# Zero-padded low parts of queries, attention heads in pairs, and the gate projected inside its attention

## The chip, the core and the metric

The kernel runs on one core of a Trainium2 chip. TensorE (PE in the profile) multiplies; VectorE (DVE), ScalarE (ACT) and GpSimd (POOL) do the rest; SyncE (SP) and ACT issue transfers. The metric is device microseconds of one execution, lower is better.

## What is computed

Two transformer blocks of two layers each, 1024 features, batch 1: a latent segment of 512 tokens and a context segment of 256. The first block has an RWKV7 layer (a recurrence over tokens) and then a differential attention layer; each layer of the second block has a feed-forward half step, a mixer of four kinds of heads (one kind is latent attention), and another half step. The change touches the two attentions. In short:

```python
# differential attention, 8 heads of 2 components of 64 features, values of 128
q, k = rope(rms_norm(proj_q)), rope(rms_norm(proj_k))     # [T, 8, 2, 64]
s = einsum("bqhcd,bkhcd->bchqk", q, k_all) * 64**-0.5      # 512 queries, 768 keys
p = softmax(s); attn = p[:, 0] - lam * p[:, 1]
y = rms_norm(einsum("bhqk,bkhe->bqhe", attn, v_all), subln) * (1 - lam_init)
y = (y * silu(proj_g)) @ w_out

# latent attention, 4 heads, 64 + 32 rotary features, values of 64
q = rms_norm(cq) @ w_uq                                    # cq has 192 features
k, v = split(rms_norm(ckv) @ w_ukv)                        # ckv has 128 features
o = softmax(q @ k_all.T * 96**-0.5) @ v_all
```

## The kernel before

Large products run on pairs of a high part and a low part in a rounded type (`fp32r`): `mm3` (L89) issues three products for each piece (high x high, high x low, low x high), and a `WStream` (L64) loads a piece of weights, lets ACT make its high part and DVE or POOL its low part. The smaller products run on plain fp32; the trace has two records for each of those, one for a transpose and one for an `fp32r` product. In the trace a form like `64*128 64x512` says that 64 rows by 128 columns of the PE array are used, for 512 columns streamed.

**Differential attention** is `da_heads` (L766). For each of 8 heads j, `queries_keys(j)` (L835) projects queries (`psq`) and keys (`psk`), norms and rotates them. The two components have 64 features each. For component c, `qq[:, c]` holds the high part of the query on all 128 rows, twice; `kk[:, c]` holds the high part of the keys on the component's own 64 rows and the low part on the other 64. So one product over 128 rows gives high x (high + low). The low part of the query, `ql`, has both components stacked, and its product takes only the 64 rows of the component:

```python
nc.tensor.matmul(o, qq[:, c, qc], kk[:, c, k0 : k0 + kn], start=True, stop=False)         # L919
nc.tensor.matmul(o, ql[cpn, qc], kk[cpn, c, k0 : k0 + kn], start=False, stop=True)        # L920
```

The keys' norm factors (`rk`, 12 columns) are spread over rows by 12 products of 64 columns of the array into `bck`. At its end `queries_keys` projects the gate (`psg`, 24 products of 512 columns, then tanh on ACT). `attend(j)` (L901) has, for each half of the queries (q2), two blocks of 128: scores, maximum on DVE (L921), exponential on ACT (L925), the weighted difference of both components on DVE (L930, L931), six transposes (`ptr`, L936), high and low parts of them, and then 18 products with the values (`po`). `values(g)` (L816) projects the values of two heads. The program writes, for each j, `values` of the pair, `queries_keys(j)`, and then `attend(j - 1)`.

**Latent attention** is `mix_attention` (L1371), called by `mix` (L1113) once for the context (layer 0 alone) and in both layers for the latent tokens. For each of 4 heads, `prepare` makes queries (`psuq`: a product over 128 rows and one over 64) and keys (`psuk`, 64 columns of the array), and `attend` takes blocks of 128 queries: scores (`pssc`), softmax, transposes (`mptr`), and the product with the values (`mpo`, 64 columns of the array, six products over 256 queries). For latent tokens two heads are in flight; for the context one.

**What sets the order.** The program is built with a planner that simulates the engines and writes every engine's instructions in an order of its own; the code's order is only where it starts, and buffers bound what it may move. The context segment of the second block (names with a `c`: `chi`, `clo`, `cx`; its feed-forward products are `pab` and `pf`) does not depend on the first block and is spread by the planner over the recurrence (about 500 to 1,600 us) and the differential attention (1,750 to 2,390 us). The latent mixers of the two layers run at about 2,867 to 3,046 and 3,860 to 4,075 us, beside projections of their other heads (`psz`, `pssv`, `psf`, `psfo`) and the output projection (`pf`).

Of the kernel before, what the change touches and what calls it, by code (L numbers as in the profile page):

```python
# [153 lines left out]
def ada(S, which, l, pool, psp, bufs=3, cols=None):  # L154
    """modulation vectors, 1024 columns at a time -> S.mod[(which, l)]; a generator of pieces"""
# [25 lines left out]
def make_gs(S, dst, mcols, gname, l):  # L181
    """dst[:, k, j] = g[k] * (1 + scale[k, j])"""
# [67 lines left out]
        # mixing factors  # L250
# [93 lines left out]
def rwkv_streams(S, st):  # L344
    """-> tw (the low-rank inputs, to be filled) and stage1(j, k, r): a generator that leaves the streams and the triangular inverses of the head pair j in DRAM"""
# [35 lines left out]
    def stage1(j, k_, r_):  # L381
# [5 lines left out]
        for hf in range(2):  # L387
# [18 lines left out]
            for d in range(2):  # L406
# [40 lines left out]
                # strictly triangular system matrices  # L447
# [81 lines left out]
def rwkv_scan(S, s1, start, fill):  # L529
    nc, tc, A = S.nc, S.tc, S.A  # L530
    with ExitStack() as st:
# [28 lines left out]
        # [.., pair of chunks, L | R, 4 blocks of 64]: L = I k k I for an odd and an even chunk, R = P r r P for an even and an odd one  # L560
# [7 lines left out]
        def group(j, d, c0, El):  # L568
            """transition matrices of the four chunks from c0 on"""
# [62 lines left out]
        def loadV(j, gi):  # L632
            """[.., direction, pair of chunks, parity, (head, v)]: V and the incoming states"""
# [10 lines left out]
        def stage2(j):  # L644
# [42 lines left out]
            # readout  # L687
# [48 lines left out]
def rwkv_out(S):  # L736
    """output projection, residual, x and context -> S.d_x (feature-major)"""
# [25 lines left out]
# ---------------------------------------------------------------- differential attention layer  # L763


def da_heads(S):  # L766
    """reads S.d_x, leaves the gated heads in S.d_yda"""
    nc, tc, A = S.nc, S.tc, S.A
    with ExitStack() as st:
# [16 lines left out]
        with tc.tile_pool(reuse_waits="tile", name="dax", bufs=1) as xp:  # L786
# [5 lines left out]
            # lambda  # L792
# [42 lines left out]
        def queries_keys(j):  # L835
            """q, k normed and roped, the gate: -> tiles for attend(j)"""
# [29 lines left out]
            ql = tp.tile([128, NLAT], F32R, tag="ql", name="ql", bufs=2)  # L866
            kk = tp.tile([128, 2, NT], F32R, tag="kk", name="kk", bufs=2)
            for t in (qs, ks[:, NCTX:]):
# [6 lines left out]
                if t is qs:  # L875
                    for c in range(2):
# [15 lines left out]
            # gate  # L892
# [3 lines left out]
            th = tp.tile([128, NLAT], F32, tag="th", name="th", bufs=2)  # L896
            nc.scalar.activation(out=th, in_=pg, func=AF.Tanh, scale=0.5)
            nc.vector.scalar_tensor_tensor(out=th, in0=th, scalar=1.0, in1=pg, op0=ALU.add, op1=ALU.mult)
            return qq, ql, kk, rq, th

        def attend(j, qq, ql, kk, rq, th):  # L901
# [3 lines left out]
            for q2 in range(2):  # L905
                PTh = ap.tile([128, 6, 256], F32R, tag="PTh", name="PTh")
                PTl = ap.tile([128, 6, 256], F32R, tag="PTl", name="PTl")
                for qi in range(2):
# [5 lines left out]
                    for c in range(2):  # L914
                        cpn = slice(64 * c, 64 * c + 64)
# [8 lines left out]
                        e = ap.tile([128, NT], F32, tag=f"e{c}", name=f"e{c}", bufs=2)  # L924
# [8 lines left out]
                    for i0 in (0, 3):  # L933
# [4 lines left out]
                        split(S, PTh[:, i0 : i0 + 3, ql_], PTl[:, i0 : i0 + 3, ql_], pv)  # L938
                q2s = slice(256 * q2, 256 * q2 + 256)
# [34 lines left out]
class Path:  # L974
    """one token segment of the second block: n tokens, modulation column j (0 latent, 1 context)"""
# [5 lines left out]
def halves(P, n, count, name):  # L981
    """count accumulators of n columns, two to a bank where they fit"""
# [8 lines left out]
def da_out(S, E, tp, after):  # L991
    """output projection and residual of the attention layer, for the latent tokens"""
# [9 lines left out]
def project(S, E, src, gate, after=None, x=None, order=range(8)):  # L1002
    """x += gate * (h @ w), 1024 features to 1024"""
# [5 lines left out]
def add(S, E, src, x, kc, gate, order, after=None):  # L1009
    """x += gate * (h @ w); before a norm, half of the features in token halves, so that the norm of one runs beside the other"""  # L1010
# [12 lines left out]
def ffn(S, E, l, which, hook=None, after=None):  # L1023
    """x += gate * swiglu(h) with h = hi + lo"""
# [34 lines left out]
class Norm:  # L1059
    """the norm of the latent tokens by halves"""  # L1060
# [21 lines left out]
class Final(Norm):  # L1082
    """the last norm, to the output"""
# [18 lines left out]
def gelu2(S, dst, ps, n, tp, bufs=True):  # L1102
    """2 * gelu(ps) (tanh form)"""
# [9 lines left out]
def mix(S, E, l):  # L1113
    """the mixed heads of one segment: hi + lo (normed input) -> hi + lo (heads, before the output projection)"""
# [7 lines left out]
    with ExitStack() as st:  # L1122
# [4 lines left out]
        def keep(name, w=n):  # L1127
            """a projection that a mixer needs later: context ones wait in DRAM"""
# [22 lines left out]
        # latent and key projections  # L1151
# [6 lines left out]
        if not kv_only:  # L1158
            cq0, cq1 = keep("cq0"), keep("cq1")
            sq0 = tp.tile([128, n], F32, tag="t0", name="sq0", bufs=2)  # L1160
            sq1 = tp.tile([128, n], F32, tag="a0", name="sq1")

# [19 lines left out]
        if not kv_only:  # L1182
            away("cq0", cq0)
            if not lat:
                nc.sync.dma_start(S.d_st["cq1"][0:64, :n], cq1[0:64])
            pss = E.at.tile([128, 512], F32, "mm", "pssq")
            for i in range(nt):
                tk = slice(128 * i, 128 * i + 128)
                mm(nc, pss[:, i : i + 1], sq0[:, tk], S.ones[:, 0:1], True, False)
                mm(nc, pss[:, i : i + 1], sq1[0:64, tk], S.ones[0:64, 0:1], False, True)  # L1190
# [3 lines left out]
        # rope of the shared key part  # L1194
# [37 lines left out]
        # pooling input  # L1232
# [10 lines left out]
        # gating units  # L1243
# [23 lines left out]
        # Fourier input  # L1267
# [7 lines left out]
        def put(ch, ps, scale=None):  # L1275
            """columns of the mixed heads, split for the output projection"""
# [10 lines left out]
        # pooling mixer  # L1287
# [24 lines left out]
        # spatial gating  # L1312
# [27 lines left out]
        # Fourier mixer  # L1340
# [30 lines left out]
def mix_attention(S, E, l, zp, tp, cq0, cq1, ckv, kr, rq, mcs, nk, fetch):  # L1371
# [7 lines left out]
    if not lat:  # L1379
        cq1 = zp.tile([128, n + 32], F32, tag="fb", name="cq1f")[:, :n]  # L1380
        nc.sync.dma_start(cq1[0:64], S.d_st["cq1"][0:64, :n])
# [9 lines left out]
    for i in range(nb):  # L1391
        kt = kr if i == 0 else zp.tile([128, NK], F32, name="mk")
        if i:
            nc.vector.tensor_copy(kt[64:96, :], kr[64:96, :])
        kts.append(kt)

    def prepare(hh):
        """the queries and keys of a head"""
        wuq = tp.tile([128, 2, 128], F32, tag=tag("wuq", "w1"), name="wuq", bufs=nb)
        nc.sync.dma_start(wuq, A["wuq"][l][:, :, 128 * hh : 128 * hh + 128])  # L1400
# [495 lines left out]
```

## Time and profile before

| | |
|---|---|
| median of 3 runs (lowest, highest) | 4460.86 us (4459.17, 4468.64) |
| span of the profiled execution | 4460.2 us |
| PE busy | 4203.0 us (94%) |
| DVE, ACT, POOL busy | 2410.0, 1633.5, 1502.2 us (54%, 37%, 34%) |
| mean granted PE clock | 0.961 of 2.4 GHz |

The profiled execution lies inside the range of the runs, and its span is 0.7 us below their median, so what lies around the span is left out. A duration in the trace is that of one instruction; matmuls overlap, so what a product costs PE is the distance from its start to the next start. A row of the timeline merges neighbours of one kind ("x16"), from the first start to the last end.

### The profile page before, as it was taken

Reading aid. Unit: us, or ns where it says so; the run is one execution under the profiler, and the core shown is the slowest. Engines: PE = TensorE matmul, PEld = TensorE weight load, DVE = VectorE, ACT = ScalarE, POOL = GpSimd, SP = SyncE. Lnnn points to the kernel's source line nnn. Section 1 sums busy time; section 2 is a strip of 40 time slices with the busy share of each in tenths; the row PEclk is TensorE's granted clock in tenths of the full one; section 3 lists DMA queues with packets and bytes.
Section 4 is the critical chain, followed back from the end, with each engine's and each line's share of the span. In section 5 each row is a group of like instructions: output and inputs, shape, how many; then the busy total and the mean of one; then the engine's idle time right before and its main releaser. Section 6 shows DMA issues by size and latency. Waiting matters only on the chain.

```text
span 4460.2 us, 70923 instructions
## 1 busy us (share of the span) xinstructions
PE 4203.0 (94%) x27642; PEld 3466.0 (78%) x27642; DVE 2410.0 (54%) x4716; ACT 1633.5 (37%) x3020; POOL 1502.2 (34%) x1187
## 2 busy tenths in 40 slices
PE   7999888999999997999998999999999999999998
PEld 5667767889768897778877888867888888857887
DVE  4677888645655435566665535554333523555434
ACT  3333333334424443444443323343222322343222
POOL 3444445356414752332223333211222222301221
PEclk9999978999999998999998999999999999999999
DMA  7775455565876653222214333311332232301332
GB/s 254 255 241 162 127 169 165 176 200 183 271 251 202 219 186 105 67 74 68 75 45 144 103 107 96 122 46 47 95 96 95 94 95 92 117 29 60 102 99 81
DMA packets 347119, 581.42 MB, mean 130 GB/s; under 512 B 96416, under 2 KB 194720, under 8 KB 345632
## 3 DMA queue, kind: packets, MB, share of 16 engines
q1 hardware_dynamic: 205856, 402.31, 28.1%
q10 hardware_dynamic: 140928, 174.58, 12.8%
q8 instruction: 218, 3.57, 0.3%
q14 instruction: 117, 0.96, 0.1%
HBM read 509.26 MB, written 67.50 MB: 129 GB/s over the span
## 4 chain that ended last, share of the span: by engine, by line
PE 78%; DVE 14%; DMA 4%; issue 2%; ACT 2%; POOL 0%; SPq 0%; ACTq 0%; DVEq 0%; POOLq 0%
PE pab L90 9%; PE pab L91 9%; PE pab L92 9%; PE pf L90 6%; PE pf L91 6%; PE pf L92 6%; PE aps L47 2%; PE ps L47 2%; DVE tmp L478 2%; DVE B L479 2%; PE pch L47 2%; PE psg L47 1%; PE psw L47 1%; PE psu L90 1%; PE mpo L47 1%
## 5 line engine op out<-in xcount | busy, mean ns | idle before, releaser
L81 POOL TENSOR_TENSOR wl<-wr,wh 128x512 fp32r<-128x512 f32 (+3 forms) x719 | 1090.4, 1527 | 2293.2 <-ACT wh L78 2100.7
L78 ACT ACTIVATE wh<-wr 128x512 fp32r<-128x512 f32 (+3 forms) x918 | 696.8, 766 | 1490.0 <-PE pab L91 585.7
L91 PE MATMUL pab<-llo,wh 128*128 128x512 f32 (+1 forms) x1472 | 561.4, 382 | 3.8 <-DVE llo L141 3.8
L90 PE MATMUL pab<-lhi,wh 128*128 128x512 f32 (+1 forms) x1472 | 557.9, 382 | 6.6 <-ACT lhi L139 6.5
L92 PE MATMUL pab<-lhi,wl 128*128 128x512 f32 (+1 forms) x1472 | 560.1, 381 | 0.0
L90 PE MATMUL pf<-gh,wh 128*128 128x256 f32 (+1 forms) x1328 | 451.9, 343 | 33.3 <-DVE cx L1018 20.1
L91 PE MATMUL pf<-gl,wh 128*128 128x256 f32 (+1 forms) x1328 | 449.2, 340 | 0.5 <-DVE gl L151 0.4
L92 PE MATMUL pf<-gh,wl 128*128 128x256 f32 (+1 forms) x1328 | 448.9, 341 | 0.9 <-POOL wl L81 0.9
L81 DVE TENSOR_TENSOR wl<-wr,wh 128x1024 fp32r<-128x1024 f32 (+2 forms) x199 | 237.6, 1195 | 211.1 <-ACT wh L78 209.0
L90 PE MATMUL pab<-chi,wh 128*128 128x256 f32 x1056 | 314.5, 299 | 18.3 <-DVE nt L138 8.6
L91 PEld LDWEIGHTS pab<-llo,wh 128*128 128x128 f32 x1472 | 278.9, 189 | 57.2 <-DVE llo L141 4.5
L90 PEld LDWEIGHTS pab<-lhi,wh 128*128 128x128 f32 x1472 | 276.9, 189 | 59.7 <-ACT lhi L139 7.9
L92 PEld LDWEIGHTS pab<-lhi,wl 128*128 128x128 f32 x1472 | 279.0, 190 | 52.3
L92 PE MATMUL pab<-chi,wl 128*128 128x256 f32 x1056 | 308.7, 295 | 6.5 <-POOL wl L81 6.1
L90 PEld LDWEIGHTS pf<-gh,wh 128*128 128x128 f32 x1328 | 254.9, 193 | 71.7 <-issue 16.8
L91 PE MATMUL pab<-clo,wh 128*128 128x256 f32 x1056 | 308.4, 293 | 0.0
L91 PEld LDWEIGHTS pf<-gl,wh 128*128 128x128 f32 x1328 | 256.5, 193 | 33.0 <-issue 1.7
L92 PEld LDWEIGHTS pf<-gh,wl 128*128 128x128 f32 x1328 | 256.2, 193 | 29.5 <-POOL wl L81 1.1
L90 PEld LDWEIGHTS pab<-chi,wh 128*128 128x128 f32 x1056 | 209.7, 199 | 32.3 <-issue 15.7
L1044 DVE TENSOR_TENSOR fth<-fth,pab 128x512 f32<-128x512 f32 (+1 forms) x154 | 88.0, 572 | 260.6 <-PE pab L92 258.7
L1018 DVE SCALAR_TENSOR_TENSOR x<-pf,lgt,x 128x512 f32<-128x512 f32 (+1 forms) x144 | 98.9, 690 | 233.9 <-PE pf L92 233.6
L1043 DVE SCALAR_TENSOR_TENSOR fth<-fth,pab 128x512 f32<-128x512 f32 (+1 forms) x154 | 87.7, 569 | 250.6 <-ACT fth L1042 250.2
(504 smaller groups left out, 9014.2 us busy)
## 6 DMA issues: line engine op xcount, KB each, us to landing
adaw<-in_adaw SPq DMA_DIRECT2D x192, 512.0 KB, 5.4
wr<-in_w SPq DMA_DIRECT2D x176, 512.0 KB, 3.5
wr<-in_w ACTq DMA_DIRECT2D x344, 256.0 KB, 3.0
wr<-in_w SPq DMA_DIRECT2D x96, 384.0 KB, 3.2
wr<-in_rwin SPq DMA_DIRECT2D x32, 512.0 KB, 5.0
wr<-in_w ACTq DMA_DIRECT2D x104, 128.0 KB, 2.1
dS<-strm SPq DMA_DIRECT2D x32, 384.0 KB, 2.7
dL<-str SPq DMA_DIRECT2D x32, 384.0 KB, 3.2
```

The source lines that it names most:

```text
L47: nc.tensor.matmul(out, lhsT, rhs, start=start, stop=stop)
L78: nc.scalar.activation(out=hv, in_=rv, func=AF.Copy)
L81: eng.tensor_tensor(out=lv, in0=rv, in1=hv, op=ALU.subtract)
L90: nc.tensor.matmul(ps, whi, xhi, start=first, stop=False)
L91: nc.tensor.matmul(ps, whi, xlo, start=False, stop=False)
L92: nc.tensor.matmul(ps, wlo, xhi, start=False, stop=last)
L478: el.tensor_tensor(out=tv, in0=B[L, 0:s, s : s + 1].to_broadcast([96, s, n]), in1=B[L, s : s + 1, s + 1 :].to_broadcast([96, s, n]), op=AL ...
L479: el.tensor_tensor(out=B[L, 0:s, s + 1 :], in0=B[L, 0:s, s + 1 :], in1=tv, op=ALU.add)
L1018: S.nc.vector.scalar_tensor_tensor(out=E.x[:, f, sl], in0=ps[:, sl], scalar=gate[:, f : f + 1], in1=E.x[:, f, sl], op0=ALU.mult, op1=ALU.add)
L1043: nc.vector.scalar_tensor_tensor(out=th, in0=th, scalar=1.0, in1=pa, op0=ALU.add, op1=ALU.mult)
L1044: nc.vector.tensor_tensor(out=th, in0=th, in1=pb, op=ALU.mult)
```

## The change

It does six things.

- `ql` gets a tile for each component's own rows, with zeros on the other 64 rows (set once, on POOL); the low product runs over all 128 rows. There are as many products of the same widths as before.
- The norm factors of the keys are first copied 64 times each into a tile of 768 columns (`spread`, one ACT instruction for each head), which six transposes bring to `bck`, in place of 12 products.
- The gate is projected by a new function `gate(j)`, called in `attend(j)` between the first half's softmax and its product with the values. `values` is called after `attend(j - 1)`, with two buffers instead of three.
- Latent attention takes two heads at a time: one product gives the keys of both (128 columns of the array), and the products with the values alternate between the two heads, one writing rows 0 to 63 of `mpo`, the other 64 to 127. Both halves are then copied out together.
- `cq1` and its square are padded with zeros from 64 to 128 rows.
- In `norm_mod` the tile `nh` has as many buffers as `nsq`, or shares its buffer where there is one. The copy of the shared key part moves from DVE to POOL.

```diff
+def spread(S, pool, cols, n, tag):
+    w = pool.tile([128, n, 64], F32, tag=tag, name="wide")
+    S.nc.scalar.activation(out=w, in_=cols.unsqueeze(2).to_broadcast([128, n, 64]), func=AF.Copy)
+    return w.rearrange("p n r -> p (n r)")
...
-            h = pool.tile([128, w], F32, tag="nh", name="nh")[:, :n]
+            h = pool.tile([128, w], F32, tag="nsq" if bufs == 1 else "nh", name="nh", bufs=bufs)[:, :n]
...
+        qls = [tp.tile([128, 2, NLAT], F32R, name=f"ql{i}") for i in range(2)]
+        for t in qls:
+            for c in range(2):
+                nc.gpsimd.memset(t[64 - 64 * c : 128 - 64 * c, c].bitcast(F32), 0.0)
...
-            vs = [[tp.tile([128, 6, 128], F32R, tag=t, name=t, bufs=3) for t in ("vh", "vl")] for _ in range(2)]
+            vs = [[tp.tile([128, 6, 128], F32R, tag=t, name=t, bufs=2) for t in ("vh", "vl")] for _ in range(2)]
...
-                        nc.vector.tensor_tensor(out=ql[own], in0=qs[own], in1=qq[own, c], op=ALU.subtract)
+                        nc.vector.tensor_tensor(out=ql[own, c], in0=qs[own], in1=qq[own, c], op=ALU.subtract)
+            wide = spread(S, tp, rk, 12, "sq")
...
-                    for h in range(2):
-                        mm(nc, bc[64 * h : 64 * h + 64, 128 * (i - i0) : 128 * (i - i0) + 128], rk[:, 2 * i + h : 2 * i + h + 1].to_broadcast([128, 64]), S.ident, True, True)
+                    nc.tensor.transpose(bc[:, 128 * (i - i0) : 128 * (i - i0) + 128], wide[:, 128 * i : 128 * i + 128], S.ident)
...
+        def gate(j):
             wg = W.load(A["dain"][3 * j + 2], 8, 128)
...
-                            nc.tensor.matmul(o, ql[cpn, qc], kk[cpn, c, k0 : k0 + kn], start=False, stop=True)
+                            nc.tensor.matmul(o, ql[:, c, qc], kk[:, c, k0 : k0 + kn], start=False, stop=True)
...
+                if q2 == 0:
+                    th = gate(j)
...
-                if j % 2 == 0:
-                    values(j // 2)
                 ts.append(queries_keys(j))
             if j:
                 attend(j - 1, *ts[j - 1])
+            if j < 8 and j % 2 == 0:
+                values(j // 2)
...
-        mm(nc, ps, wuq[0:64, 1, :], cq1[0:64], False, True)
+            mm(nc, ps, wuq[:, 1, :], cq1, False, True)
...
-            mm(nc, ps[0:64, :w], wukv[:, 64 * hh : 64 * hh + 64], ckv[:, t0 : t0 + w], True, True)
-            nc.scalar.activation(out=kt[0:64, t0 : t0 + w], in_=ps[0:64, :w], func=AF.Copy)
+            mm(nc, ps[:, :w], wukv[:, 128 * p : 128 * p + 128], ckv[:, t0 : t0 + w], True, True)
+            for h in range(2):
+                nc.scalar.activation(out=two[h][0:64, t0 : t0 + w], in_=ps[64 * h : 64 * h + 64, :w], func=AF.Copy)
...
-            PT = tp.tile([128, nk, 256], F32, tag="PT", name="mPT", bufs=nb)
+            for h in range(2):
+                PT = tp.tile([128, nk, 256], F32, tag=f"PT{h}", name="mPT")
...
             for i in range(nk):
-                mm(nc, po[op], V[:, i, 64 * hh : 64 * hh + 64], PT[:, i, :], i == 0, i == nk - 1)
+                for h in range(2):
+                    mm(nc, po[64 * h : 64 * h + 64], V[:, i, 128 * p + 64 * h : 128 * p + 64 * h + 64], PTs[h][:, i, :], i == 0, i == nk - 1)
```

How the planner now orders the engines, at two places. On PE, in the first head of the differential attention, the spreading of the key factors (`bck`) stood, with filler of the context's feed-forward (`pab`) ahead of it, directly before the gate (`psg`):

```order
L92 MATMUL pab<-chi,wl 128x256
L47 MATMUL bck<-ident,rk 64x128 x12
L90 MATMUL psg<-dhi,wh 128x512
L91 MATMUL psg<-dlo,wh 128x512
L92 MATMUL psg<-dhi,wl 128x512
```

Now filler stands on both sides of it:

```order
L91 MATMUL pab<-clo,wh 128x256
L898 MATMUL bck<-ident,wide 128x128 x6
L92 MATMUL pab<-chi,wl 128x256
L90 MATMUL pab<-chi,wh 128x256
L91 MATMUL pab<-clo,wh 128x256
```

Six transposes have taken the place of the twelve products, and the gate no longer follows them. Later on PE, in the attention of the head, the gate now stands behind a score product:

```order
L933 MATMUL scores<-kk,qq 128x512
L934 MATMUL scores<-kk,ql_19572 128x512
L933 MATMUL scores<-kk,qq 128x256
L90 MATMUL psg<-dhi,wh 128x512
L91 MATMUL psg<-dlo,wh 128x512
L92 MATMUL psg<-dhi,wl 128x512
```

The 24 products moved from ahead of the head's scores to behind the third product of the seventh of its eight groups of four score products.

On PE at the end of the first latent mixer of the second block, the transposes and value products of the last two heads came one head after the other:

```order
L91 MATMUL pf<-al,wh 128x512
L92 MATMUL pf<-ah,wl 128x512
L1445 MATMUL mptr<-ident,me 128x128 x9
L47 MATMUL mpo<-mPT,mV 64x256 x6
L1445 MATMUL mptr<-ident,me 128x128 x12
L47 MATMUL mpo<-mPT,mV 64x256 x6
```

Now the two heads' products with the values stand together, and 21 transposes in a row ahead of the last of them:

```order
L47 MATMUL mpo<-mPT,mV 64x256 x12
L1467 MATMUL mptr<-ident,me 128x128 x3
L47 MATMUL pssc<-mk,mq 128x512
L47 MATMUL pssc<-mk,mq 128x256
L92 MATMUL pf<-lhi,wl 128x512
L90 MATMUL pf<-ah,wh 128x512
L91 MATMUL pf<-al,wh 128x512
L92 MATMUL pf<-ah,wl 128x512
L1467 MATMUL mptr<-ident,me 128x128 x21
L47 MATMUL mpo<-mPT,mV 64x256 x12
```

So the value products of two heads moved behind the transposes of both, and four output products (`pf`) are the only other work between the last two groups of them.

## Rows read from the trace of the kernel before

**Rows 1.** Page, block 4: the chain that ended last, share by engine.

```profile
PE 78%; DVE 14%; DMA 4%; issue 2%; ACT 2%; POOL 0%; SPq 0%; ACTq 0%; DVEq 0%; POOLq 0%
```

**Rows 2.** Busy time by stretch: length, PE, PEld, DVE, ACT, POOL, clock, DMA share, GB/s.

```profile
500.00:1150.00 650.00, 596.74 (x5860) 521.40 (x5858) 452.50 (x992) 250.96 (x540) 321.10 (x308) 0.91 0.59 179
1760.00:2390.00 630.00, 590.75 (x3680) 498.47 (x3681) 393.98 (x898) 279.89 (x550) 199.13 (x165) 0.95 0.22 68
2925.00:3046.00 121.00, 117.16 (x516) 71.40 (x515) 61.75 (x123) 51.11 (x108) 7.36 (x4) 1.00 0.08 26
```

**Rows 3.** Waits of PE, 1760 to 2390 us: total, times, longest.

```profile
PE pf L90 <- DVE cx L1018: 14.6, 10, 3.9
PE ptr L936 <- DVE e L931: 6.8, 5, 3.3
```

**Rows 4.** Timeline of PE, scores of the first component: start, duration, instruction.

```profile
1818.18 0.40 PE L92 MATMUL psq<-dhi,wl 128*128 128x512 f32 x1
1818.41 0.40 PE L919 MATMUL scores<-kk,qq 128*128 128x512 f32 x1
1818.74 0.49 PE L920 MATMUL scores<-kk,ql 64*128 64x512 f32 x1
1819.16 0.38 PE L919 MATMUL scores<-kk,qq 128*128 128x256 f32 x1
1819.47 0.38 PE L920 MATMUL scores<-kk,ql 64*128 64x256 f32 x1
1819.79 0.38 PE L90 MATMUL pab<-chi,wh 128*128 128x256 f32 x1
1820.01 0.28 PE L91 MATMUL pab<-clo,wh 128*128 128x256 f32 x1
1820.13 0.28 PE L92 MATMUL pab<-chi,wl 128*128 128x256 f32 x1
```

**Rows 5.** The same for the second component: its first product, and what follows its last.

```profile
1832.31 0.36 PE L919 MATMUL scores<-kk,qq 128*128 128x256 f32 x1
...
1833.77 0.38 PE L90 MATMUL pab<-chi,wh 128*128 128x256 f32 x1
```

**Rows 6.** Timeline of PE: spreading of key factors in one head, and six transposes.

```profile
1803.34 1.09 PE L47 MATMUL bck<-ident,rk 128*64 128x128 f32 x16 [2.10 <-DVE rk L61]
1804.74 0.66 PE L47 MATMUL bck<-ident,rk 128*64 128x128 f32 x8 [0.31 <-DVE tr L872]
...
1843.21 0.87 PE L936 MATMUL ptr<-ident,e 128*128 128x128 f32 x6 [1.51 <-DVE e L931]
```

**Rows 7.** Timeline of PE: products on 32, 64 and 128 columns of the array.

```profile
79.44 1.50 PE L47 MATMUL aps<-adaw,silc 128*32 128x256 f32 x24
...
2931.59 2.08 PE L47 MATMUL psuq<-cq,wuq 128*128 128x512 f32 x4
...
2936.94 1.07 PE L47 MATMUL psuk<-ckv,wukv 128*64 128x512 f32 x2
...
2939.60 0.65 PE L47 MATMUL psuk<-ckv,wukv 128*64 128x256 f32 x2
...
2951.62 2.80 PE L47 MATMUL mpo<-mPT,mV 128*64 128x256 f32 x12
...
3004.68 7.03 PE L47 MATMUL psfo<-dft,pf 128*128 128x512 f32 x16
```

**Rows 8.** The tile `mpo`: all its products.

```profile
L47 PE MATMUL mpo<-mPT,mV x208: 379/379/623, 1235.1 to 4032.7; 128*64 128x256 f32 x104
```

**Rows 9.** Softmax on ACT and DVE in 2925 to 3046 us: count, busy us, mean ns.

```profile
L1438 ACT ACTIVATE me<-pssc,mmx,mrq 128x768 f32<-128x768 f32 x16 | 15.9, 993 | 0.1
L1446 ACT ACTIVATE mPT<-mptr 128x384 f32<-128x384 f32 x28 | 12.9, 489 | 10.2 <-PE mptr L1445 9.8
L1434 DVE TENSOR_REDUCE mmx<-pssc 128x1 f32<-128x768 f32 x16 | 15.2, 956 | 8.8 <-PE pssc L47 8.7
```

**Rows 10.** The tile `pch` of the recurrence: copies of its results that are written first.

```profile
L681 DVE COPY O<-pch x96: 269/285/296, 600.0 to 1433.3; 64x128 f32<-64x128 f32 x96
```

More of the change, by code (lines that the diff above doesn't have):

```diff
@@ L865, in queries_keys @@
             qq = tp.tile([128, 2, NLAT], F32R, tag="qq", name="qq", bufs=2)
-            ql = tp.tile([128, NLAT], F32R, tag="ql", name="ql", bufs=2)
+            ql = qls[j % 2]
             kk = tp.tile([128, 2, NT], F32R, tag="kk", name="kk", bufs=2)
@@ L1184, in mix @@
             if not lat:
[L1185 removed]
+                nc.sync.dma_start(S.d_st["cq1"][:, :n], cq1)
             pss = E.at.tile([128, 512], F32, "mm", "pssq")
@@ L1189, in mix @@
                 mm(nc, pss[:, i : i + 1], sq0[:, tk], S.ones[:, 0:1], True, False)
-                mm(nc, pss[:, i : i + 1], sq1[0:64, tk], S.ones[0:64, 0:1], False, True)
+                mm(nc, pss[:, i : i + 1], sq1[:, tk], S.ones[:, 0:1], False, True)
             rq = zp.tile([128, nt], F32, name="mrq")
@@ L1390, in mix_attention @@
     kts = []
-    for i in range(nb):
+    for i in range(2):
         kt = kr if i == 0 else zp.tile([128, NK], F32, name="mk")
         if i:
-            nc.vector.tensor_copy(kt[64:96, :], kr[64:96, :])
+            nc.gpsimd.tensor_copy(kt[64:96, :], kr[64:96, :])
         kts.append(kt)
-    def prepare(hh):
-        wuq = tp.tile([128, 2, 128], F32, tag=tag("wuq", "w1"), name="wuq", bufs=nb)
-        nc.sync.dma_start(wuq, A["wuq"][l][:, :, 128 * hh : 128 * hh + 128])
-        qt = tp.tile([128, n], F32, tag=tag("mq", "a0"), name="mq", bufs=nb)[0:96]
-        kt = kts[hh % nb][0:96]
-        ps = halves(P, n, 1, "psuq")[0]
-        mm(nc, ps, wuq[:, 0, :], cq0, True, False)
-        mm(nc, ps, wuq[0:64, 1, :], cq1[0:64], False, True)
-        if not lat:
-            nc.scalar.activation(out=qt, in_=ps[0:96], func=AF.Copy)
-        else:
-            nc.scalar.activation(out=qt[0:64], in_=ps[0:64], func=AF.Copy)
-            t2 = tp.tile([128, n], F32, tag="mrt", name="mrt")
-            nc.vector.tensor_tensor(out=t2[64:96], in0=ps[96:128], in1=mcs[96:128, 1, :], op=ALU.mult)
-            nc.vector.tensor_tensor(out=qt[64:96], in0=ps[64:96], in1=mcs[64:96, 0, :], op=ALU.mult)
-            nc.vector.tensor_tensor(out=qt[64:96], in0=qt[64:96], in1=t2[64:96], op=ALU.add)
@@ new lines, in prepare @@
+    def prepare(p):
+        qts = []
+        for hh in (2 * p, 2 * p + 1):
+            wuq = tp.tile([128, 2, 128], F32, tag=tag("wuq", "w1"), name="wuq", bufs=nb)
+            nc.sync.dma_start(wuq, A["wuq"][l][:, :, 128 * hh : 128 * hh + 128])
+            qt = tp.tile([128, n], F32, tag=f"mq{hh % 2}", name="mq")[0:96]
+            ps = halves(P, n, 1, "psuq")[0]
+            mm(nc, ps, wuq[:, 0, :], cq0, True, False)
+            mm(nc, ps, wuq[:, 1, :], cq1, False, True)
+            if not lat:
+                nc.scalar.activation(out=qt, in_=ps[0:96], func=AF.Copy)
+            else:
+                nc.scalar.activation(out=qt[0:64], in_=ps[0:64], func=AF.Copy)
+                t2 = tp.tile([128, n], F32, tag="mrt", name="mrt")
+                nc.vector.tensor_tensor(out=t2[64:96], in0=ps[96:128], in1=mcs[96:128, 1, :], op=ALU.mult)
+                nc.vector.tensor_tensor(out=qt[64:96], in0=ps[64:96], in1=mcs[64:96, 0, :], op=ALU.mult)
+                nc.vector.tensor_tensor(out=qt[64:96], in0=qt[64:96], in1=t2[64:96], op=ALU.add)
+            qts.append(qt)
+        two = [kt[0:96] for kt in kts]
@@ new lines, in prepare, with attend @@
+            mm(nc, ps[:, :w], wukv[:, 128 * p : 128 * p + 128], ckv[:, t0 : t0 + w], True, True)
+            for h in range(2):
+                nc.scalar.activation(out=two[h][0:64, t0 : t0 + w], in_=ps[64 * h : 64 * h + 64, :w], func=AF.Copy)
+        return qts, two
+    def attend(p, qts, two):
+        for q2 in range(0, n, 256):
+            PTs = []
+            for h in range(2):
+                PT = tp.tile([128, nk, 256], F32, tag=f"PT{h}", name="mPT")
+                for qb in range(2):
+                    qc = slice(q2 + 128 * qb, q2 + 128 * qb + 128)
+                    ps = P.tile([128, 1024], F32, "sc", "pssc") if lat else P.tile([128, 512], F32, "mm", "pssc")
+                    for k0 in range(0, NK, 512):
+                        k1 = min(NK, k0 + 512)
+                        mm(nc, ps[:, k0:k1], qts[h][:, qc], two[h][:, k0:k1], True, True)
+                    sv = ps[:, :NK]
+                    mx = tp.tile([128, 2], F32, tag="mmx", name="mmx", bufs=2)
+                    nc.vector.tensor_reduce(out=mx[:, 0:1], in_=sv, axis=AX.X, op=ALU.max)
+                    rc = rq[:, q2 // 128 + qb : q2 // 128 + qb + 1]
+                    nc.vector.scalar_tensor_tensor(out=mx[:, 0:1], in0=mx[:, 0:1], scalar=-1.0, in1=rc, op0=ALU.mult, op1=ALU.mult)
+                    e = tp.tile([128, NK], F32, tag=tag("me", "a1"), name="me", bufs=nb)
+                    nc.scalar.activation(out=e, in_=sv, func=AF.Exp, scale=rc, bias=mx[:, 0:1], accum_out=mx[:, 1:2])
+                    nc.vector.reciprocal(out=mx[:, 1:2], in_=mx[:, 1:2])
+                    nc.vector.tensor_scalar(out=e, in0=e, scalar1=mx[:, 1:2], scalar2=None, op0=ALU.mult)
+                    for i0 in range(0, nk, 3):
+                        ni = min(3, nk - i0)
+                        pt = P.tile([128, 512], F32, "mm", "mptr")
+                        for i in range(ni):
+                            nc.tensor.transpose(pt[:, 128 * i : 128 * i + 128], e[:, 128 * (i0 + i) : 128 * (i0 + i) + 128], S.ident)
+                        nc.scalar.activation(out=PT[:, i0 : i0 + ni, 128 * qb : 128 * qb + 128], in_=pt[:, : 128 * ni].rearrange("p (i q) -> p i q", i=ni), func=AF.Copy)
+                PTs.append(PT)
@@ L1447, in attend @@
             po = P.tile([128, 512], F32, "mm", "mpo")[:, :256]
             for i in range(nk):
-                mm(nc, po[op], V[:, i, 64 * hh : 64 * hh + 64], PT[:, i, :], i == 0, i == nk - 1)
-            hq, lq = E.ah[op, ch, q2 : q2 + 256], E.al[op, ch, q2 : q2 + 256]
-            nc.scalar.activation(out=hq, in_=po[op], func=AF.Copy)
-            nc.vector.tensor_tensor(out=lq, in0=po[op], in1=hq, op=ALU.subtract)
-    ready = []
-    for hh in range(5):
-        if hh < 4:
-            ready.append((hh, *prepare(hh)))
-        if ready and (len(ready) == nb or hh == 4):
-            attend(*ready.pop(0))
+                for h in range(2):
+                    mm(nc, po[64 * h : 64 * h + 64], V[:, i, 128 * p + 64 * h : 128 * p + 64 * h + 64], PTs[h][:, i, :], i == 0, i == nk - 1)
@@ L1462 @@
+            hq, lq = E.ah[:, p, q2 : q2 + 256], E.al[:, p, q2 : q2 + 256]
+            nc.scalar.activation(out=hq, in_=po, func=AF.Copy)
+            nc.vector.tensor_tensor(out=lq, in0=po, in1=hq, op=ALU.subtract)
+    for p in range(2):
+        attend(p, *prepare(p))
 class Heads:
```

39 lines of the change are left out of this document (8 added, 31 removed).

## Prediction, made before the changed kernel ran

> **What bounds the kernel now.** I read the chain that ended last first: PE holds 78% of it, DVE 14% and ACT 2% [rows 1]. So a microsecond that PE saves counts as long as PE stays what is waited for, and the next views ask that of the two stretches which the change touches. The busy time by stretch says that in the differential attention (1,760 to 2,390 us) PE is busy 590.75 of 630 us and DVE 393.98, ACT 279.89; in the first latent mixer (2,925 to 3,046 us) PE is busy 117.16 of 121 us and DVE 61.75, ACT 51.11 [rows 2]. PE is the bound of both, with 39 and 4 us idle, and DVE, next in line, has slack of more than a third. The waits of PE in the differential attention name what it stands idle for: 14.6 us for `cx` of the filler, and 6.8 us for the softmax's `e` [rows 3]. Both are small beside the stretch: the softmax is hidden, and the cost of a product on PE is what I add up. The trace's span is 4460.2 us, 0.7 us under the median of the runs, so I subtract from 4460.2 and call the result a median.
>
> **The low products of the scores.** The neighbours of full rows run from start to start in 0.23 us for 512 columns (1818.18 to 1818.41) and 0.12 us for 256 (1820.01 to 1820.13) [rows 4]. Four score products would then take 2 x (0.23 + 0.12) = 0.70 us. They take 1819.79 - 1818.41 = 1.38 us for the first component [rows 4] and 1833.77 - 1832.31 = 1.46 us for the second [rows 5]. The steps from the full product to the 64-row one and back are all long, 0.31 to 0.42 us [rows 4], with no wait shown between them. What the padded product has in common with the full ones is its 128 rows, so I take 0.70: a saving of 0.72 on average, for 8 heads x 4 blocks x 2 components = 64 groups, 46 us. From below it is bounded by nothing, if the price is not one of the rows (a rival below). The zeros are set once on POOL, before the stretch in which POOL is busy 199 of 630 us [rows 2]; the subtractions that fill `ql` are as many as before.
>
> **The key factors.** For one head the products into `bck` take 1.09 + 0.66 = 1.75 us, where six transposes over the whole array take 0.87 [rows 6]: 0.88 x 8 = 7 us. `spread` is new on ACT, 768 columns, so about the 0.99 us of an exponential of that width [rows 9], 8 us over the heads. ACT has 350 us of slack in the stretch, and filler stands on PE ahead of the transposes in the order shown, so I cost it at nothing; without that cover it is 8 us.
>
> **The latent attention.** Products with the values (`mpo`): 208 records [rows 8], 12 in 2.80 us, 0.233 each [rows 7], together 48.5 us. That two such products on different halves of the columns run side by side is shown by two rows: 24 `aps` products of 256 columns on a quarter of the columns take 1.50 us, 0.0625 each, against 0.22 over the whole array (half of `psfo`'s 0.44 for 512 columns) [rows 7], and the 16 records of `bck`, which alternate between halves, 1.09 us [rows 6], 0.07 each, no more than half of a transpose's 0.145 [rows 6]. So I take half, 24 us; from below the bound is nothing saved, if the two halves wait for each other. Keys (`psuk`): a pair of records of 512 columns takes 1.07 us, of 256 columns 0.65 [rows 7]; there are 8 and 12 of them, 8 x 1.07 + 12 x 0.65 = 16.4 us. In their place come half as many products over the full array, at the price of `psfo`, 7.03 / 16 = 0.44 a record of 512 columns [rows 7]: 4 x 0.88 + 6 x 0.44 = 6.2. Saved, 10 us. Queries: `psuq`, one product of 64 rows among two, 2.08 us for four records, against 4 x 0.44 = 1.76 [rows 7]: 0.32 x 8 heads in two layers = 2.6 us.
>
> For the halves there is a rule that speaks against it. The Trainium skill ("TensorE: Matmul & The Clock Gate", section "Measured speedup vs the span model") lists 2.38 times for three tiles of columns, not 3. By that share two halves would give some 1.59 times (an estimate from that page), `mpo` would keep 30.5 of 48.5 us, and the sum would be 6 us smaller. The rows of `aps` show four tiles at a quarter of the price each, so the sum goes by them.
>
> **What moves.** The gate's 24 products of 512 columns (24 x 0.23 = 5.5 us a head) move behind scores of their own head. In the head shown they stand between the third and the fourth product of a group of scores, so that group's softmax comes 5.5 us later; its block's transposes then wait, with queries of the next head (`psq`) on PE to fill the time. The values come after the previous head's attention and have two buffers in place of three: loads and high parts may start later; PE's longest waits before are for other things [rows 3]. `nh` with two buffers can only take a wait away, and the key copy goes to POOL, which is the idlest there [rows 2]. All these I cost at nothing, since PE waits 39 us in all of the stretch and the order keeps filler (`pab`, `pf`) between; uncovered, the gate costs 5.5 us in each of 8 heads, 44 us.
>
> **What is given back.** With PE faster, the softmax is later relative to it. In the latent mixer each softmax costs DVE 0.96 us and ACT 0.99 + 2 x 0.49 us [rows 9], and at the end PE has two heads' transposes in a row (21, at 0.145 = 3.0 us) with four output products (0.9 us) as its only cover in the new order. A pair thus ends with about one softmax, 0.96 + 0.99 us, for which PE waits: 2 us x 2 pairs x 2 layers = 8 us. In the differential attention the wait for `e` of 6.8 us may grow by a third, 2 us. Both together 10 us, between 0 and 40 (the idle 39 us of that stretch doubled).
>
> Sum: 46 + 7 + 24 + 10 + 2.6 = 90 us saved, 10 given back: 4460.2 - 90 + 10 = **4380 us**. The main case lies between 4355 (nothing given back, and the clock of rival two half regained) and 4410 (40 given back).
>
> **Rivals.** (1) *The softmax becomes the bound.* Each block of scores goes through maximum, exponential and difference before its transposes, and if PE waits for these, the faster scores only make it wait longer: the 46 us are lost, 4426 us. For it: DVE is the second busiest, and a gate inside a group of scores. Against it: DVE is busy 63% of the stretch [rows 2] and the waits for `e` are 6.8 us [rows 3]. (2) *The clock rises.* The granted clock is 0.95 of 2.4 GHz in the differential attention [rows 2]; if steadier use of the whole array keeps it at 1.00, 5% of 630 us = 31 us come on top, 4349 us. Against it: PE is already busy 94% there, and after the saving it waits more. (3) *The padding saves nothing*, since the long steps come not from the 64 rows but from two products that write the same place one after the other, or from the weights' load. Then `psuq` saves nothing either: 4380 + 46 + 2.6 = 4429 us. Against it: `psq` products also follow each other into one place, with new weights each time, at 0.23 us [rows 4]. The Trainium skill has a rule on that side ("TensorE: Matmul & The Clock Gate", section "The mechanism"): loads of weights overlap with running products only where the group of rows differs. By it, padded products could not load ahead and the time would be this rival's; the row of `psq`, whose full products come every 0.23 us, disagrees. (4) *The recurrence gets slower.* The order of PE is rearranged there too, though no work changes: other filler stands ahead of the serial results. If each of the 96 results copied first [rows 10] waits behind 12 more filler products, 12 x 0.12 = 1.4 us, that is 138 us if PE then lacks filler later: 4380 + 138 = 4518 us. It decides from 80 / 96 = 0.83 us, seven products, each. For it: the clock (0.91) and the idle time, 53 us of 650, are worst there [rows 2]. Against it: the filler is as much as before, so what stands earlier is missing later and PE does the same work.
>
> **How the numbers follow.** Main case .67; rival (1) .13; (2) .10; (3) .04; (4) .06. The range from 4345 to 4430 takes in the main case and the first three and leaves out (4) and tails. Within 0.2% (9 us, about what a measurement of this kernel can tell from no change) the time would have to be over 4452: the weak part of (4) and the upper tails, .04. Slower by more: the rest of (4), .05. Faster: .91.
>
> **What would show it.** Right: in the trace of after, a group of four score products from start to start in 0.7 us (1.38 refutes the step and makes (3) true); 12 `mpo` records in 1.4 us (2.8: the halves don't run side by side); six `bck` transposes in 0.87 us. The busy time of PE in the differential attention some 50 us less with idle time still near 39; if idle time is near 85 there, (1) holds. A granted clock over 0.97 there speaks for (2). The recurrence's end moved by more than 10 us speaks for (4). In the latent mixers, a new wait of PE for `mPT` or `me` of about 2 us at the end of each pair is the 8 us given back; none makes the time 4372. What would make me wrong most simply is the order: a planner that uses the saved time to put other work in rows where it collides, which only the trace of after tells.

## The result, and the profile after

The changed kernel takes 4408.51 us (median of 4 runs, 4395.81 to 4421.83) where the kernel before takes 4464.75; the ratio is 0.9881, 95% interval 0.9857 to 0.9906. Measured again beside other variants it was 0.9883 (0.9867 to 0.9899). It is faster by 56 us (50 when measured again), inside the range, and 28 us slower than the likeliest case.

From the page of the changed kernel, whose span is 4408.5 us (busy us, share of the span, instructions):

```profile
PE 4116.0 (93%) x27478; PEld 3447.1 (78%) x27478; DVE 2399.9 (54%) x4704; ACT 1637.3 (37%) x3018; POOL 1516.9 (34%) x1200
```

The chain that ended last can be followed back only to some 732 us here (its shares, PE 70% and DVE 8% first, add up to 83%), so it can't be set beside [rows 1]; what follows goes by stretches. PE's busy time fell from 4203.0 to 4116.0 us: 87 saved, 90 were forecast. Its idle time rose from 4460.2 - 4203.0 = 257 to 4408.5 - 4116.0 = 292 us: 35 given back, 10 were forecast. So the shortfall is nearly all in what is given back. Between the same points of the program, PE's idle time rose by 16 us in the differential attention, by 12 in the recurrence (870 - 818.46 = 51.5 to 878 - 814.98 = 63.0) and by 7 in the two latent mixers. By stretch (the columns as in [rows 2]; the differential attention, the first latent mixer):

```profile
1763.00:2356.00 593.00, 537.90 (x3519) 485.22 (x3520) 401.33 (x900) 285.97 (x555) 200.35 (x163) 0.95 0.22 71
2896.00:3012.00 116.00, 107.24 (x544) 72.25 (x544) 60.09 (x124) 53.66 (x111) 7.47 (x4) 0.99 0.09 28
```

In the differential attention PE is busy 53 us less and idle 593 - 537.90 = 55 us, where it was 39. The clock stayed at 0.95. Some waits of PE there (total, times, longest), to be read beside [rows 3]:

```profile
PE bck L898 <- ACT wide L111: 6.3, 4, 2.8
PE ptr L950 <- DVE e L945: 6.2, 4, 3.3
PE scores L933 <- ACT e L939: 5.7, 5, 2.1
PE pf L90 <- DVE cx L1034: 2.9, 3, 1.4
```

The wait for `wide` is new: it is the copy that I costed at nothing (the products before waited 2.6 us for `rk`). The wait of the scores for the exponential (`e` on ACT, which frees the score buffer) was not among my rows; before it was

```profile
PE scores L919 <- ACT e L925: 1.7, 3, 0.8
```

The wait of the transposes for `e`, which I had expected to grow, stayed (6.8 to 6.2), and the largest wait before, 14.6 us of the filler for `cx`, shrank. So the 16 us are the balance of many rows, and no single wait explains them.

The score products of one component, in the timeline of the changed kernel (start, duration), against [rows 4]:

```profile
1823.28 0.39 PE L933 MATMUL scores<-kk,qq 128*128 128x512 f32 x1
1823.51 0.39 PE L934 MATMUL scores<-kk,ql 128*128 128x512 f32 x1
...
1823.97 0.28 PE L90 MATMUL pab<-chi,wh 128*128 128x256 f32 x1
```

From 1823.28 to 1823.97 are 0.69 us, where they were 1.38. Six `bck` transposes take 0.82 to 0.88 us in four heads and 1.18 to 1.54 in the other four, so the eight heads save some 6 us (7 forecast). In the latent mixer, the value products of two heads at once; then the transposes at the end of the mixer:

```profile
2934.13 2.81 PE L47 MATMUL mpo<-mPT,mV 128*64 128x256 f32 x24
...
3004.41 0.84 PE L1467 MATMUL mptr<-ident,me 128*128 128x128 f32 x6 [1.79 <-DVE me L1462]
3005.79 0.84 PE L1467 MATMUL mptr<-ident,me 128*128 128x128 f32 x6 [0.54 <-DVE me L1462]
```

24 records take 2.81 us from the first start to the last end, 0.117 each, where 12 took 2.80, 0.233 each [rows 7]: the halves of the columns run side by side at half the price. The transposes at the end wait 1.79 + 0.54 us for the softmax, as forecast.

The third place with more idle time is the recurrence. All `pch` products before, then after (first and last start):

```profile
L47 PE MATMUL pch<-ZV,G x768: 217/275/476, 592.3 to 1459.6; 128*128 128x64 f32 x192
```

```profile
L47 PE MATMUL pch<-ZV,G x768: 217/275/475, 591.1 to 1468.2; 128*128 128x64 f32 x192
```

The same 768 records take 867 us before and 877 after, in one execution each; the changed kernel's second profile has 887.

### The profile page after: what moved, and what is told of

It is laid out like the page before. It is cut to its first block, busy times and chain, and to the rows that moved or that the text cites. A ratio compares the mean times of both kernels' runs of the same rounds, so it can differ in the third digit from the quotient of the medians.

```text
span 4408.5 us, 70611 instructions
## 1 busy us (share of the span) xinstructions
PE 4116.0 (93%) x27478; PEld 3447.1 (78%) x27478; DVE 2399.9 (54%) x4704; ACT 1637.3 (37%) x3018; POOL 1516.9 (34%) x1200
## 4 chain that ended last, share of the span: by engine, by line
PE 70%; DVE 8%; DMA 2%; ACT 2%; issue 1%; POOL 0%; ACTq 0%; SPq 0%; DVEq 0%; POOLq 0%
PE pab L91 9%; PE pab L90 9%; PE pab L92 9%; PE pf L90 6%; PE pf L91 6%; PE pf L92 6%; PE psg L47 2%; PE pch L47 2%; PE ps L47 1%; PE psz L91 1%; PE aps L47 1%; PE pssc L47 1%; PE psz L90 1%; PE psz L92 1%; DMA adaw<-in_adaw 1%
```

## Experiments

Twelve runs; a variant of the changed kernel is compared with its 4408 to 4411 us, one of the kernel before with 4461 to 4466.

| kernel | median us | ratio to before (95%) |
|---|---|---|
| changed, low products on 64 rows | 4449.87 | 0.9974 (0.9962 to 0.9985) |
| changed, gate in `queries_keys` | 4403.17 | 0.9864 (0.9849 to 0.9878) |
| changed, values early, two buffers | 4475.62 | 1.0031 (1.0019 to 1.0043) |
| changed, values early, three buffers | 4605.28 | 1.0312 (1.0297 to 1.0328) |
| changed, key factors by twelve products | 4406.06 | 0.9869 (0.9851 to 0.9887) |
| changed, `nh` in one buffer of its own | 4407.51 | 0.9870 (0.9856 to 0.9884) |
| changed, gate and key factors as before | 4412.25 | 0.9883 (0.9863 to 0.9902) |
| changed, gate as before and `nh` | 4411.30 | 0.9887 (0.9872 to 0.9901) |
| changed, once more | 4410.83 | 0.9883 (0.9867 to 0.9899) |
| before, padding alone | 4616.96 | 1.0344 (1.0326 to 1.0362) |
| before, latent attention alone | 4449.94 | 0.9962 (0.9949 to 0.9974) |
| before, 1 KB unused | 4666.46 | 1.0460 (1.0444 to 1.0476) |

**The padding undone.**

```diff
-nc.tensor.matmul(o, ql[:, c, qc], kk[:, c, k0 : k0 + kn], start=False, stop=True)
+nc.tensor.matmul(o, ql[64 * c : 64 * c + 64, c, qc], kk[64 * c : 64 * c + 64, c, k0 : k0 + kn], start=False, stop=True)
```

> The changed kernel with one thing undone: the low product of the scores runs over the component's own 64 rows again (the other 64 rows of ql and their zeros stay unused). The order of every engine is the changed kernel's. Theory (the 64 rows are what made score products slow, and the time is PE's): a group of four score products takes 1.4 us again, the busy time of PE rises by 40 us, and the time by 35 to 45 us, to some 4445. Rival 1 (the softmax sets the pace in the differential attention): PE's idle time there falls by as much as the products grow, and the time rises by under 15 us. Rival 3 (padding saves nothing): groups of 0.7 us also here, the time stays within 9 us of the changed kernel's.

The time rose by 40 us. PE's row for the same part of the program, and the score group:

```profile
1766.00:2390.00 624.00, 579.18 (x3515) 488.63 (x3514) 395.50 (x888) 285.63 (x552) 198.58 (x163) 0.96 0.21 66
```

```profile
1825.44 0.39 PE L933 MATMUL scores<-kk,qq 128*128 128x512 f32 x1
1825.76 0.50 PE L934 MATMUL scores<-kk,ql 64*128 64x512 f32 x1
1826.19 0.38 PE L933 MATMUL scores<-kk,qq 128*128 128x256 f32 x1
...
1826.82 0.39 PE L90 MATMUL pab<-chi,wh 128*128 128x256 f32 x1
```

1.38 us again, in the same order of every engine: 64 rows beside 128 are what costs, and rival 3 is out. The weight loads (PEld) show where the time goes. Two loads of the variant, of a low product and of the full one behind it, then the load of a padded low product in the changed kernel:

```profile
1825.76 0.18 PEld L934 LDWEIGHTS scores<-kk,ql 64*128 64x128 f32 x1 [0.24 <-issue]
1826.19 0.19 PEld L933 LDWEIGHTS scores<-kk,qq 128*128 128x128 f32 x1 [0.25 <-issue]
```

```profile
1823.29 0.19 PEld L934 LDWEIGHTS scores<-kk,ql 128*128 128x128 f32 x1
```

With padding the load begins 0.22 us ahead of its product (1823.51). With 64 rows it begins with its product (1825.76), and the load of the full product behind it does too (1826.19), so its 0.18 us are not hidden. That holds for all the low products of the scores in the kernel before and in this variant. The 64 rows alone don't do it: in the kernel before, the second record of `psw<-tw,lw` (64 rows, plain fp32, behind its like) has its load 0.32 us ahead. So it goes with the change of rows from one product to the next.

PE is busy 41 us more and idle 624 - 579.18 = 45 us, 10 fewer than with padding (8 if the stretch is cut at the very same products). So of the 41 us that padding saves in this stretch 8 to 10 are given back in waits. Rival 1 is a quarter true at most.

**The padding alone, in the kernel before** (the two tiles, their zeros, the subtraction and the product of the change, nothing else).

> The kernel before with one part of the change alone: ql padded to 128 rows (two tiles, zeros set once), gate, values and key factors as they were. In the changed kernel the two stretches from the differential attention's start to the first latent mixer lost 52.6 us of PE's work but only 33.7 us of time, since PE's idle time there rose by 19 us. If the faster products themselves bring that idle time (the softmax takes as long as it did), it is here too: PE busy falls by 41 to 46, the time by about 30, to 4434. If the idle time comes from the moved gate and values or the spread factors, the time falls by the whole 41 to 46 us, to about 4421.

Both expectations were wrong: 151 us slower. In the differential attention (1,710 to 2,271 us) and the stretch behind it:

```profile
1710.00:2271.00 561.00, 436.94 (x2577) 375.08 (x2578) 347.22 (x844) 229.16 (x427) 69.19 (x44) 0.86 0.12 41
2272.00:3026.00 754.00, 656.39 (x3667) 575.80 (x3667) 299.16 (x512) 258.35 (x460) 287.46 (x242) 0.92 0.35 111
```

PE is idle 124 us in the first and 98 in the second, at lower clocks. The first holds not one `pab` product; before, it has three groups like this (line, tile, shape, count, busy, mean ns):

```profile
L90 PE MATMUL pab<-chi,wh 128*128 128x256 f32 x288 | 89.0, 309 | 10.3 <-DVE nt L138 7.9 <-DVE fth L1044 2.2 <-ACT wh L78 0.2
```

and in the padded kernel the second stretch has 352 of each instead. Without filler the attention's chain shows bare. PE's largest waits in it:

```profile
PE scores L923 <- ACT e L929: 31.7, 16, 5.4
PE ptr L940 <- DVE e L935: 22.6, 9, 5.7
```

The score products themselves are as fast here as in the changed kernel. But the padded tiles take 4 KB per partition more. That led to a new theory: room in memory decides whether the context's work may stand inside the attention.

**One unused tile, in the kernel before.**

```diff
+spare = tp.tile([128, 256], F32, name="spare")
+nc.gpsimd.memset(spare, 0.0)
```

> The kernel before with one unused tile of 1 KB per partition in the pool of the differential attention (set to zero once on POOL); nothing else is changed and nothing reads it. The padding alone took 152 us more than the kernel before, and its trace has no product of the context's feed-forward inside the differential attention, where the kernel before has 864 and 404 of the two kinds. If room in memory decides this (the context's tiles must wait for those of the attention), the unused tile does the same: no such product there, and 4600 to 4640 us. If the padded products or their order were the cause, the time stays within 9 us of 4464.

206 us slower, with no `pab` product inside the attention here either, and no product changed. In the attention:

```profile
1712.00:2317.00 605.00, 500.97 (x2578) 393.60 (x2578) 347.10 (x844) 229.50 (x425) 67.74 (x41) 0.82 0.12 38
```

PE is idle 104 us there, and 99 in the 756 us behind it, at granted clocks of 0.82 and 0.92. So room decides it, as far as the runs go: against the kernel before, the tiles of the attention take 1 KB more here, 4 KB with the padding alone and 2 KB in the variant with three buffers below, and these three have no `pab` product inside it; the changed kernel takes 4 KB less (4 more for `ql`, 6 less for the values, 2 less for `th`), and it and every other variant, none above the kernel before, keep theirs. By that the kernel before had less than 1 KB left. Which tiles then collide was not read. The recurrence kept 869 us; the loss is in the attention and behind it.

**Values early.** With the buffers as in the change:

```diff
+                if j % 2 == 0:
+                    values(j // 2)
                 ts.append(queries_keys(j))
...
-            if j < 8 and j % 2 == 0:
-                values(j // 2)
```

> The changed kernel with the values written ahead of queries_keys again, as before, but with the two buffers of the change. If their new place costs PE (5.6 us of waits for wh on ACT are new in the differential attention), these waits go and the time falls by about 5 us. With two buffers and the early place, the loads must wait for the head before: then it rises by 5 to 20 us. If neither decides, it stays within 9 us of 4408.

67 us slower: the rise was forecast at 20 at most. The products with the values (`po`) of two heads stand close (1,864 to 1,941 us), and the next pair's begin only at 2,045; in the changed kernel no two of its sixteen groups lie more than 46 us apart. Two buffers hold one pair of heads, so values written early must wait for the pair before to be used up: each time the last of the `psv` products begin just behind the pair's last `po` (1,944 behind 1,942 us, 2,116 behind 2,115, 2,295 behind 2,291), and the next queries stand behind them. With three buffers, as in the kernel before (`bufs=3` besides):

> The changed kernel with the values written ahead of queries_keys and with three buffers, both as before. With two buffers this place cost 67 us. If buffers were what was short, three bring the time to within 10 us of the changed kernel's 4408, and less than it if the late place of the values is what costs PE its 19 us of idle time (then about 4395). If the place itself is bad with faster scores, it stays over 4430.

197 us slower, again with no `pab` product inside the attention: 6 KB more than the change takes, 2 KB more than the kernel before. So two buffers pay for the padding, and the late place is what two buffers need.

**The gate back.** `gate`'s body at the end of `queries_keys`, two buffers for `th` (2 KB more, which still fits).

> The changed kernel with the gate projected at the end of queries_keys again (tanh result in two buffers). PE's idle time in the differential attention went from 39 to 55 us. If the moved gate is the cause (5.7 us of waits for ACT's e, 4.4 us for ks), idle time there falls back by 8 to 15 us and the time to about 4396. If the cause is that PE is simply faster beside the same softmax, the time stays within 9 us of 4408; the gate stood as cover ahead of the scores, so it could also rise by some 5 us.

4403 us; the intervals overlap, so its place is worth nothing that could be measured either way. PE's idle time in the stretch is 609 - 556.65 = 52 us, not the 40 to 47 that the gate as cause would have given. The gate between the products of a score group did no harm that shows.

**Key factors as before.**

> The changed kernel with the key factors spread by twelve products of 64 columns, without the copy on ACT. The trace of the changed kernel has a wait of 6.3 us for the copy (wide) which was forecast as hidden. If that wait eats the saving, the products into bck cost 7 us more, the wait goes, and the time stays within 5 us of the changed kernel's. If the copy is hidden after all, the time is 7 us longer.

2 to 5 us faster than the changed kernel, within the intervals. The wait for `wide` (6.3 us) is gone and 8.4 us of waits for `rk` have its place. So `bck` waits for the factors in either form; the saving on PE comes to nothing in time that could be measured.

**The latent attention alone** (`mix` and `mix_attention` of the change in the kernel before).

> The kernel before with the latent attention of the change alone (heads in pairs, padded cq1, the key copy on POOL). Theory: PE loses 38 us of work in the mixers (mpo 20.6, psuk 9.2, psuq 6, and what switching costs), each mixer gives back 3 to 4 us of waits for the softmax, and the time falls by about 30 us, to 4435. Rival: halves of the array do not run side by side; then mpo keeps its 48 us and the time falls by only 5 to 10 us.

16 us faster, not 30. PE is busy 4203.0 - 4172.9 = 30 us less (38 expected) and idle 19 more. From the first `psz` product to the last output product on `ah` the two mixers are 14 us shorter each (222.4 to 208.1 and 226.7 to 212.5), as expected, but the recurrence takes 879 us in this order, 12 more than before, with the context's mixer inside it. The halves run side by side; what is missing was lost elsewhere, most of it in the recurrence.

**`nh` in one buffer.**

```diff
-h = pool.tile([128, w], F32, tag="nsq" if bufs == 1 else "nh", name="nh", bufs=bufs)[:, :n]
+h = pool.tile([128, w], F32, tag="nh", name="nh")[:, :n]
```

> The changed kernel with nh in norm_mod in one buffer of its own again. The recurrence (first pch to last pch) takes 877 us in the changed kernel and 868 before, with the same work; the order there is another. If the freed buffer is what lets the planner write the other order, the recurrence goes back to 868 us and the time falls by about 9 us, to 4399. If the order is moved by any edit, the recurrence takes some other length between 865 and 880 us and the rest of the trace stays as it is. If nh itself gains, the norms get slower and the time rises by 3 to 10 us.

No change in time, and the recurrence took 875 us, not 868: nothing here says that `nh` is the cause.

**Two combinations, and the change again.**

> The changed kernel with two things undone together: the gate is projected in queries_keys, and the key factors are spread by twelve products. Alone they gave 4403 and 4406 us. If what they give adds up, some 4400 us. If each only moves the same waits about, it stays between 4401 and 4412.

> The changed kernel with the gate projected in queries_keys and nh in a buffer of its own. Alone they gave 4403 and 4408 us. If the order of the recurrence is moved by any edit, its length lies between 865 and 880 us here and decides the time: 4395 to 4410. A candidate for a version that beats the changed kernel.

> The changed kernel once more, so that the variants of this call have it beside them on the same chip. Expected as measured, 4408 within 5 us, with the recurrence at 877 us again if its length is fixed by the order and not by the single execution; a length near 868 would say that the 10 us were chance.

4412, 4411 and 4411 us: nothing adds up, and no version here beats the change beyond its interval. The recurrence took 878, 874 and 887 us. The last is the very program that took 877: two executions of one program are as far apart as before and after, so its length is not fixed by the order alone. Still, the changed kernel, its repetition and the variant with its very order have 877, 887 and 877, and the kernel before and its variants with the padding alone and the unused tile, which keep its order on PE in the recurrence nearly record for record, 867, 868 and 869; over all variants it is 868 to 889. That the order of the filler sets part of it is likely, not shown; which rows do it was not found.

## Why the prediction was right, and where its terms were off

- **The direction and the saving on PE** were right by their own steps. Scores: 0.69 us a group (0.70 forecast); `mpo`: half (half); PE busy in all: 87 us less (90). What neighbouring rows of full size cost was the price of the padded product. That the sum came out so close is in part luck: taken alone, the scores save 41 us (46 forecast), the latent attention 30 (37) and `bck` some 6 (7), together 77; where the other 10 come from was not found (one program's busy time differs by 5 us between two executions, 4116.0 and 4121.0).
- **Given back: 35 us, not 10.** This term was mis-sized. In the mixers it held: 7 us against 8, and `me` is waited for at the end of a pair, as the sum had it. In the differential attention 16 us came up, not 2, and in the recurrence 12, for which the sum had no term. I let one wait grow by a third, which did not grow, and did not look at the others: 8 to 10 us are the price of faster scores, shown by the variant with 64 rows; what brings the other 6 to 8 was not found.
- **`spread` costed at nothing** was wrong by 6.3 us of waits, about what the transposes save. The cover I named, filler ahead of it in the order, was not enough. The copy itself loses nothing against products in the same order, which wait 8.4 us for `rk`; in the kernel before they waited 2.6.
- **The recurrence** was rival 4, with a size far off: 10 us, not 138, and even these are no more than two executions of one program differ by. That the filler is the same and PE works while a step waits, which I said against the rival, fits.
- **Rivals 1, 2 and 3.** The first got a quarter of its 46 us at most; the clock of the second stayed at 0.95; the third is out, though the weights' load that it named is where the time goes: it is exposed because the rows change.
- **What the sum never priced is room in memory.** I costed the values' two buffers and their place, and the gate's move, at nothing. In the sum that holds, because the change has them all. But the two buffers make room for the padding, and the late place is what they need: undone, the variants are 197 and 67 us slower, and padding alone turns a gain of 40 us into a loss of 151. No rival of mine named this; had the change left 4 KB unpaid, the forecast would have failed by far.
- **The two rules of the Trainium skill** ("TensorE: Matmul & The Clock Gate"). By "Measured speedup vs the span model" two halves would have given 1.59 times (my estimate from it); the trace shows 0.233 / 0.117 = 2.0 times. By the rule on loads in "The mechanism" padding would have saved nothing; the 0.69 us disagree, and so does the load that begins 0.22 us ahead of its product. The same section of the Trainium skill also lets a load into a background buffer go ahead, which I had passed over. A rule of the Trainium skill that I left out fits: "TensorEngine Tiling (Array Packing)", section "Key Properties", says that changing the tiling mode drains the engine. Here each change between 128 and 64 rows costs (1.38 - 0.69) / 4 = 0.17 us on average, about one exposed load of 0.18 us; the drain itself no run here shows.

## What to carry to other kernels

Price an edit by the products of full size beside it, and look at whether each weight load begins ahead of its product. Then ask of every buffer that the edit adds what had that room: where work of two stages shares memory, the order on the engines shows at once whether the filler is still inside the stage. Edits that look idle (a buffer fewer, a later place) may be the payment for the one that gains, so undo them one at a time. And count what covered a wait before you take its cover away.

## What was not expected of the hardware

That a single unread kilobyte per partition costs 206 us (4460.54 to 4666.46) comes from the program's order, since no product changed, but it was the largest effect seen. Of the chip: alternating between products of 128 and of 64 rows costs PE 0.17 us each time, where the weights of the next product are loaded only when it starts (0.18 us); and two heads on halves of the columns cost no more than one (2.81 us against 2.80).
